# The gates of a hybrid layer in four groups of 32 columns, the first norm's sums in the same way, softplus on 144 columns, and another load order at the start

## The chip, the cores and the metric

The kernel runs on one core of one Trainium2 chip. The metric is the device time of one execution in microseconds; a run of it is repeated, and the median counts. Five engines are named: PE (matrix product), DVE (vector), ACT (scalar functions), POOL (a second, slower vector engine) and SP (which issues DMAs).

## What is computed

One inference step of a hybrid decoder layer on 576 tokens (512 of a new sequence, 64 new ones of eight older sequences), with D = 2048:

```
def _rmsnorm(x, g):
    y = xf * lax.rsqrt(jnp.mean(xf * xf, axis=-1, keepdims=True) + EPS)
    return y * g

x += W_out [GatedDeltaNet heads | mLSTM heads](RMSNorm(x) W_in)
x += ConvFFN(RMSNorm(x));  final RMSNorm
```

W_in gives q, k and v of 8 deltanet heads (each through a causal convolution of width 4 and silu), their output gates, the same for 4 mLSTM heads, and 24 rows of gates: 8 betas (sigmoid), 8 decays (softplus, times a coefficient), 4 input and 4 forget gates of the mLSTM (log-sigmoid). Everything behind the norm is float32.

## The kernel before

Tokens lie along the free axis, in two halves of 288; channels lie on the 128 partitions, so x is 16 tiles ("k") of 128x576. A float32 product is made of three faster ones: each operand is split into a high part (fp32r) and its remainder, and `three` (L193) issues high·high, high·low and low·high, each on two halves: three pairs of 128x288 matmuls for one k. `dense` (L202) does that for 16 k: one tile of 128 output channels. Its result lies in one of two "pd" buffers of PSUM until DVE has read it. Weights come in units of 128x1024 (8 k): `load_unit` (L123) issues the DMA on SP's queue, the cast to the high part on ACT (L120) and the subtraction on DVE (L121); a dense uses two units, in order of a list that begins with w_in's tile 0, the gates.

PE runs in the order in which the program is written. Beside the denses run jobs: generators that `spawn` registers. `tick`, at the end of each k of a dense, counts down every job, and where one is due lets it issue its next piece; `yield 14` means 14 k's later. So a piece of a job stands between two k's of a dense on PE. ACT, DVE, POOL and SP are ordered by a scheduler from priorities, ahead of time; each engine then keeps its order and waits where an operand is not there.

`startup` (L332) loads x on SP's queue and the parameters (par) on POOL's, makes the high and low parts of x times the norm's gain (L356 on ACT, L357 on DVE), squares x on ACT (L363) and adds the squares on DVE and POOL in turn (L365), with a last add L366. `gates` (L370) loads con (constants) and dnst (convolution states) on POOL's queue, fills small tables and runs the gate tile's dense as the first on PE, into two "pr" buffers of PSUM. Then `mixer` (L285) runs, for each head, the denses of q, k, v and z. Behind each of q, k and v stands `conv_in` (L525): an evacuation in three pieces, multiplied by rstd (L536 to L538), and the convolution (L543 to L551) on DVE with a tanh on ACT.

The job `gate_rows` (L404) goes on with the gates: 14 k's later the sum of squares over the partitions (L256, two matmuls with a matrix of ones, which also spreads it over all partitions), the reciprocal root (L244 on ACT, L245 to L248 on DVE) into rstd, the gates times rstd (L414), 6 k's later sigmoid and softplus on tiles of 128x576 (L419 to L446; the series L438 seven times, a reciprocal L432), 30 k's later the running sums, and 30 k's later the transposes L514 and L517 on PE, which turn the rows into columns for the heads. Each head is a job `dn_head` of its own (L585), which waits for the gates and the head before it; its inverse has L843 in it, its last steps L771 and its sample part L747, where four matmuls work side by side on four groups of 32 columns. L1004 in `ml_sample` does the same.

Of the kernel before, what the change touches and what calls it, by code (L numbers as in the profile page):

```python
# [19 lines left out]
NT = SEQ + NB * LS  # L20
HALF = NT // 2
# [9 lines left out]
EPS = 1e-6  # L31
# [37 lines left out]
class Layer:  # L69
# [214 lines left out]
    def mixer(self):  # L284
# [5 lines left out]
        for h in range(DNH):  # L290
            q, k, v = (self.conv_in(8 * i + h, self.dense()) for i in range(3))
# [40 lines left out]
    def startup(self):  # L332
        nc, I = self.nc, self.I
        self.par = self.cp.tile([P, NPAR], F32, tag="par", name="par")
        nc.gpsimd.dma_start(out=self.par, in_=I["par"])
# [7 lines left out]

        self.xh, self.xl = [], []
        acc = [self.r(), self.r()]
        xs = []
        acts = [self.new_act(k) for k in reversed(range(KT))][::-1]
        for k in range(KT):
            x = self.r()
            xs.append(x)  # L350
            nc.sync.dma_start(out=x, in_=I["xT"][k])
            if k in (1, 3):
                self.load_unit()
            hi, lo = acts[k]
            g = self.par[:, G1 + k:G1 + k + 1]
# [11 lines left out]
        self.acc = acc  # L367


    def gates(self):  # L370
# [3 lines left out]
        Pl.dma_start(out=self.con, in_=I["con"])  # L374
        self.ident = self.con[:, C_ID:C_ID + P]
        self.dnst = self.p1.tile([P, 24, 9, 3], F32, tag="dnst", name="dnst")
        Pl.dma_start(out=self.dnst, in_=I["dn_conv"])
# [28 lines left out]
    def gate_rows(self, outs):  # L406
        nc, I, O = self.nc, self.I, self.O
        V, A, Pl = nc.vector, nc.scalar, nc.gpsimd
        yield 14
        self.rms_bc(self.acc[0], self.rstd)  # L410
        gr = self.r()
        for hf in range(2):
            sl = slice(hf * HALF, (hf + 1) * HALF)
            V.tensor_tensor(out=gr[:, sl], in0=outs[hf], in1=self.rstd[:, sl], op=ALU.mult)  # L414
        yield 6
        edge = self.tc.issue_after(self.last_evac.ins)
        edge.__enter__()
        y = self.r()
        V.tensor_scalar(out=y, in0=gr, scalar1=self.par[:, GB:GB + 1], scalar2=self.con[:, C_SG:C_SG + 1], op0=ALU.add, op1=ALU.mult)  # L419
        R1, R2, R3 = self.r(), self.r(), self.r()  # L420
        for t in (R1, R2, R3):
            Pl.memset(t, 0.0)
        th = self.r()
        A.activation(th[0:8], gr[0:8], AF.Tanh, scale=0.5)
        V.tensor_scalar(out=R1[0:8], in0=th[0:8], scalar1=0.5, scalar2=0.5, op0=ALU.mult, op1=ALU.add)

        e = self.r()
        A.activation(e, y, AF.Abs)
        A.activation(e, e, AF.Exp, scale=-1.0)
        d = self.r()  # L430
# [1229 lines left out]
```

## Time and profile before

| what | value |
|---|---|
| median of 3 runs | 2697.02 us (2696.75 to 2697.04) |
| the profiled execution | 2699.44 us, its span 2697.70 us |
| granted TensorE clock over the span | 0.995 |
| PE busy | 2651.0 us, 98% |
| DVE busy | 1994.0 us, 74% |
| ACT busy | 1080.2 us, 40% |
| POOL busy | 333.6 us, 12% |
| data moved | 304.02 MB, 113 GB/s on the mean |

Read the shares last. PE is busy nearly throughout, so the question for any edit is in which of PE's few idle stretches it acts, and the views that show this are the list of PE's waits, the timelines of the engines at the start, and the busy times of single stretches.

### The profile page before, as it was taken

Reading aid. Unit: us, or ns where it says so; the run is one execution under the profiler, and the core shown is the slowest. Engines: PE = TensorE matmul, PEld = TensorE weight load, DVE = VectorE, ACT = ScalarE, POOL = GpSimd, SP = SyncE. Lnnn points to the kernel's source line nnn. Section 1 sums busy time; section 2 is a strip of 40 time slices with the busy share of each in tenths; the row PEclk is TensorE's granted clock in tenths of the full one; section 3 lists DMA queues with packets and bytes.
Section 4 is the critical chain, followed back from the end, with each engine's and each line's share of the span. In section 5 each row is a group of like instructions: output and inputs, shape, how many; then the busy total and the mean of one; then the engine's idle time right before and its main releaser. Section 6 shows DMA issues by size and latency. Waiting matters only on the chain.

```text
span 2697.7 us, 48872 instructions
## 1 busy us (share of the span) xinstructions
PE 2651.0 (98%) x19967; PEld 2607.0 (97%) x19967; DVE 1994.0 (74%) x3338; ACT 1080.2 (40%) x1704; POOL 333.6 (12%) x658
## 2 busy tenths in 40 slices
PE   7999999999999999998999999999999999999998
PEld 7998999999999999998999999999999999999998
DVE  7887777765544332389888888888888888888646
ACT  5334344443333322254444444444444433433324
POOL 3222322222211001101000000000000100000001
PEclk9999999999999999999999999999999999999999
DMA  5222222222333344444333333333333373342333
GB/s 195 85 77 87 90 91 91 91 88 92 114 113 104 115 135 135 135 123 150 107 111 108 108 108 108 108 108 108 108 108 109 109 256 94 106 146 71 122 97 100
DMA packets 112233, 304.02 MB, mean 113 GB/s; under 512 B 21912, under 2 KB 28184, under 8 KB 112008
## 3 DMA queue, kind: packets, MB, share of 16 engines
q1 hardware_dynamic: 107896, 291.17, 34.0%
q0 software_dynamic: 1872, 7.37, 0.8%
q8 instruction: 156, 2.56, 0.4%
q10 hardware_dynamic: 2240, 2.36, 0.3%
q14 instruction: 69, 0.57, 0.1%
HBM read 264.79 MB, written 36.06 MB: 112 GB/s over the span
## 4 chain that ended last, share of the span: by engine, by line
PE 89%; DVE 4%; DMA 1%; issue 0%; ACT 0%; POOL 0%; DVEq 0%; POOLq 0%; SPq 0%; ACTq 0%
PE pd L198 36%; PE pr L1283 31%; PE pd L1283 12%; PE pr L198 3%; PE pr L1509 1%; DVE bl L121 1%; DVE wl L121 1%; DMA r<-hid 0%; DVE r L1544 0%; PE pr L256 0%; PE pr L843 0%; PE pr L980 0%; PE pr L982 0%; PE pr L690 0%; PE pr L687 0%
## 5 line engine op out<-in xcount | busy, mean ns | idle before, releaser
L120 ACT CAST wh<-raw 128x1024 fp32r<-128x1024 f32 (+1 forms) x394 | 404.6, 1027 | 741.1 <-PE pd L198 400.2
L1283 PE MATMUL pr<-bh,wh 128*128 128x288 f32 x2120 | 626.8, 296 | 1.9 <-ACT bh L120 1.9
L1283 PE MATMUL pr<-bh,wl 128*128 128x288 f32 x2120 | 624.6, 295 | 0.5 <-DVE wl L121 0.5
L1283 PE MATMUL pr<-bl,wh 128*128 128x288 f32 x2120 | 624.3, 294 | 0.6 <-DVE bl L121 0.6
L121 DVE TENSOR_TENSOR wl<-raw,wh 128x1024 fp32r<-128x1024 f32 (+1 forms) x394 | 476.5, 1210 | 178.8 <-ACT wh L120 172.4
L198 PE MATMUL pd<-ah,wh 128*128 128x288 f32 x2496 | 560.3, 306 | 0.0
L198 PE MATMUL pd<-ah,wl 128*128 128x288 f32 x2496 | 534.5, 296 | 0.2 <-DVE wl L121 0.2
L198 PE MATMUL pd<-al,wh 128*128 128x288 f32 x2496 | 533.8, 296 | 0.0
L198 PEld LDWEIGHTS pd<-ah,wh 128*128 128x128 f32 x2496 | 401.0, 189 | 14.2 <-issue 7.7
L198 PEld LDWEIGHTS pd<-ah,wl 128*128 128x128 f32 x2496 | 401.8, 189 | 0.5 <-DVE wl L121 0.5
L198 PEld LDWEIGHTS pd<-al,wh 128*128 128x128 f32 x2496 | 401.7, 189 | 0.0
L1283 PEld LDWEIGHTS pr<-bl,wh 128*128 128x128 f32 x2120 | 400.0, 189 | 1.1 <-DVE bl L121 1.1
L1283 PEld LDWEIGHTS pr<-bh,wh 128*128 128x128 f32 x2120 | 398.4, 188 | 2.1 <-ACT bh L120 2.1
L1283 PEld LDWEIGHTS pr<-bh,wl 128*128 128x128 f32 x2120 | 398.9, 188 | 1.2 <-DVE wl L121 1.2
L120 ACT CAST wh<-s 128x1024 fp32r<-128x1024 f32 (+1 forms) x171 | 169.6, 992 | 361.2 <-DVE s L1248 142.2
L1283 PE MATMUL pd<-bh,wh 128*128 128x288 f32 x848 | 252.2, 297 | 5.6 <-ACT wh L120 5.6
L1283 PE MATMUL pd<-bh,wl 128*128 128x288 f32 x848 | 250.8, 296 | 1.7 <-DVE wl L121 1.7
L1283 PE MATMUL pd<-bl,wh 128*128 128x288 f32 x848 | 249.7, 294 | 0.0
L121 DVE TENSOR_TENSOR wl<-s,wh 128x1024 fp32r<-128x1024 f32 (+1 forms) x171 | 196.5, 1149 | 26.0 <-ACT wh L120 18.4
L1283 PEld LDWEIGHTS pd<-bh,wh 128*128 128x128 f32 x848 | 160.3, 189 | 6.1 <-ACT wh L120 6.1
L1283 PEld LDWEIGHTS pd<-bh,wl 128*128 128x128 f32 x848 | 160.6, 189 | 2.2 <-DVE wl L121 2.2
L1283 PEld LDWEIGHTS pd<-bl,wh 128*128 128x128 f32 x848 | 161.0, 190 | 0.0
(400 smaller groups left out, 3501.1 us busy)
## 6 DMA issues: line engine op xcount, KB each, us to landing
raw<-in_w_up SPq DMA_DIRECT2D x176, 512.0 KB
raw<-in_w_in SPq DMA_DIRECT2D x114, 512.0 KB
raw<-in_w_down SPq DMA_DIRECT2D x40, 512.0 KB
raw<-in_w_out SPq DMA_DIRECT2D x32, 512.0 KB
raw<-in_w_down SPq DMA_DIRECT2D x40, 384.0 KB
hid<-r SPq DMA_DIRECT2D x44, 288.0 KB
r<-hid SPq DMA_DIRECT2D x40, 288.0 KB
r<-in_xT SPq DMA_DIRECT2D x32, 288.0 KB
```

The lines of the kernel that those rows point to most:

```text
L120: nc.scalar.copy(hi, src)
L121: nc.vector.tensor_tensor(out=lo, in0=src, in1=hi.bitcast(F32), op=ALU.subtract)
L198: mm(outs[hf], w, x[:, hf * HALF:(hf + 1) * HALF], start=first and i == 0, stop=last and i == 2)
L1283: mm(out, w[:, ks], x[:, sl], start=k == 0 and i == 0, stop=k == nk - 1 and i == 2)
L1509: mm(pr[:, 0:n], w[:, ks], acts[kk][:, a * NT + sl.start:a * NT + sl.stop], start=kk == 0 and i == 0, stop=kk == FB - 1 and i == 2)
```

## The change

The gates no longer have a dense of their own. Tile 0 of w_in is read once as four float32 tiles of 128x512 (4 k's each, L371), of which POOL takes the 32 columns that matter, scaled by the norm's gain (L372), to `gw`. Their product is made in float32 on x itself, in 16 k's of four matmuls, one for each quarter of the tokens (144), into four groups of 32 output rows of one PSUM buffer (L422): inside q's dense of head 0, in blocks of four k's. Behind each k ACT squares x in place (L423). The sums of the squares are made in the same shape with 32 columns of ones (L431), in four blocks inside k's dense. The reciprocal root then runs on 128x144. One row of each group is copied to a wide tile (L436), which two matmuls with ones spread to all partitions (L452), and ACT copies that to rstd (L453). Sigmoid and softplus run on 128x144 (L465 to L487), with coefficients per group (cq, made by a small matmul L456), and two matmuls with a selection matrix (`there`, L496) bring the four groups back to rows of 576, 9 k's behind L456. For head 0, q's and k's denses now both stand ahead of the two `conv_in`. On SP's queue the first unit of q's weights stands ahead of x and the second behind four tiles of x; par, con and dnst move to this queue, and a slice of par with the norm's gain (g1) goes first on POOL's.

The core of the diff (the softplus' own steps and the memsets are left out; they are the same steps on another shape):

```diff
-        for name, n in (("w_in", NIN), ("w_out", KT), ("w_up", 2 * NPL - 2)):
-            for t in range(n):
+        for name, t0, n in (("w_in", 1, NIN), ("w_out", 0, KT), ("w_up", 0, 2 * NPL - 2)):
+            for t in range(t0, n):
...
-            q, k, v = (self.conv_in(8 * i + h, self.dense()) for i in range(3))
+            if h == 0:
+                pds = [self.dense(), self.dense()]
+                q, k = (self.conv_in(8 * i, pd) for i, pd in enumerate(pds))
+            else:
+                q, k = (self.conv_in(8 * i + h, self.dense()) for i in range(2))
+            v = self.conv_in(16 + h, self.dense())
...
-        nc.gpsimd.dma_start(out=self.par, in_=I["par"])
+        g1 = self.r(shape=[P, KT])
+        nc.gpsimd.dma_start(out=g1, in_=I["par"][:, G1:G1 + KT])
...
         for k in range(KT):
+            if k in (0, 8):
+                self.load_unit()
             x = self.r()
-            xs.append(x)
+            self.xs.append(x)
             nc.sync.dma_start(out=x, in_=I["xT"][k])
-            if k in (1, 3):
-                self.load_unit()
...
-        for k in range(KT):
-            e = nc.gpsimd if k % 2 else nc.vector
-            sq = acc[k] if k < 2 else self.r()
-            nc.scalar.activation(sq, xs[k], AF.Square)
-            if k > 1:
-                e.tensor_tensor(out=acc[k % 2], in0=acc[k % 2], in1=sq, op=ALU.add)
-        nc.vector.tensor_tensor(out=acc[0], in0=acc[0], in1=acc[1], op=ALU.add)
+            if k % 4 == 3:
+                self.gate_weights(k - 3, g1)
+        nc.sync.dma_start(out=self.par, in_=I["par"])
+
+    def gate_weights(self, k, g1):
+        raw = self.r(shape=[P, 4, 4, 32])
+        self.nc.sync.dma_start(out=raw, in_=self.I["w_in"][0][k // 8][:, k % 8 * P:(k % 8 + 4) * P].rearrange("p (k g w) -> p k g w", k=4, g=4))
+        self.nc.gpsimd.tensor_tensor(out=self.gw[:, k:k + 4].rearrange("p k (g w) -> p k g w", g=4), in0=raw[:, :, :, 0:8],
+                                     in1=g1[:, k:k + 4].unsqueeze(2).unsqueeze(3).to_broadcast([P, 4, 4, 8]), op=ALU.mult)
...
-        outs = [self.psr()[:, 0:HALF] for _ in range(2)]
-        self.dense(outs)
-        return self.spawn(self.gate_rows(outs))
+        return self.spawn(self.gate_rows())
...
-        yield 14
-        self.rms_bc(self.acc[0], self.rstd)
...
-        yield 6
+        yield 3
+        for k in range(KT):
+            for s, t in quarters:
+                mm(pg[s], self.gw[:, k], self.xs[k][:, t], start=k == 0, stop=k == KT - 1)
+            A.activation(self.xs[k], self.xs[k], AF.Square)
+            if k in (3, 7, 11):
+                yield 4
+        ps = self.psr()[:, 0:Q]
+        for k in range(KT):
+            if k % 4 == 0:
+                yield 1 if k == 0 else 4
+            for s, t in quarters:
+                mm(ps[s], self.ones[:, 0:32], self.xs[k][:, t], start=k == 0, stop=k == KT - 1)
+        self.rsqrt_bc([(ps, slice(0, Q))], 1.0 / D, self.eps6, EPS, rq[:, 0], rq[:, 1], rq[:, 2])
+        for j, (s, t) in enumerate(quarters):
+            (A.copy if j % 2 else V.tensor_copy)(wide[32 * j:32 * j + 1, t], rq[32 * j:32 * j + 1, 0])
...
+        yield 3
+        for sl in halves:
+            pr = self.psr()[:, 0:HALF]
+            mm(pr, self.ones, wide[:, sl], start=True, stop=True)
+            A.copy(self.rstd[:, sl], pr)
+        yield 4
+        pc = self.psr()
+        mm(pc[:, 0:6], back.rearrange("p j g w -> p (j g w)"), cs, start=True, stop=True)
...
-        yield 30
+        yield 9
+        for sl in halves:
+            pr = self.psr()[:, 0:HALF]
+            mm(pr, there.rearrange("p g w -> p (g w)"), t5[:, sl], start=True, stop=True)
+            A.copy(sp[:, sl], pr)
+        A.copy(R1[0:8], sp[0:8])
+        yield 5
...
-        yield 30
+        yield 26
```

Three places in the engines' orders follow. The first is ACT while x arrives: `ah` is the high part of a tile of x (ah_123 is the first, ah_93 the last), `wh` that of a unit of weights. Before, after the second cast:

```order
L120 CAST wh_147<-raw_145 128x1024
L356 ACTIVATE ah_115<-r_153,par 128x576
L356 ACTIVATE ah_113<-r_157,par 128x576
L356 ACTIVATE ah_111<-r_161,par 128x576
L356 ACTIVATE ah_109<-r_165,par 128x576
L356 ACTIVATE ah_107<-r_169,par 128x576
L356 ACTIVATE ah_105<-r_173,par 128x576
L356 ACTIVATE ah_103<-r_177,par 128x576
L356 ACTIVATE ah_101<-r_181,par 128x576
L356 ACTIVATE ah_99<-r_185,par 128x576
L363 ACTIVATE r_91<-r_125 128x576
```

After, from the second cast on:

```order
L120 CAST wh_171<-raw_169 128x1024
L541 COPY mp_900<-par 4x8
L360 ACTIVATE ah_115<-r_150,r_83 128x576
L360 ACTIVATE ah_113<-r_154,r_83 128x576
L423 ACTIVATE r_131<-r_131 128x576
L423 ACTIVATE r_135<-r_135 128x576
L423 ACTIVATE r_139<-r_139 128x576
L423 ACTIVATE r_143<-r_143 128x576
L360 ACTIVATE ah_111<-r_158,r_83 128x576
L360 ACTIVATE ah_109<-r_162,r_83 128x576
L360 ACTIVATE ah_107<-r_175,r_83 128x576
```

The four squares L423 now stand between the scalings, each behind the gate matmuls that read the same tile; before, the first square L363 came behind nine scalings of this stretch and no PE instruction.

The second place is PE at the end of head 0's k tile, with the sum's last block (16 matmuls), the two that spread the result (L452) and the first of v's dense (pd_678). Before, L256 stood a k ahead of the end of q's dense (pd_388), and k's dense (pd_528) began behind it:

```order
L198 MATMUL pd_388<-ah_95,wh_336 128x288 x2
L198 MATMUL pd_388<-al_96,wh_336 128x288 x2
L198 MATMUL pd_388<-ah_95,wl_337 128x288 x2
L256 MATMUL pr_491<-r_91,ones 128x288
L256 MATMUL pr_493<-r_91,ones 128x288
L198 MATMUL pd_388<-ah_93,wh_336 128x288 x2
L198 MATMUL pd_388<-al_94,wh_336 128x288 x2
L198 MATMUL pd_388<-ah_93,wl_337 128x288 x2
L198 MATMUL pd_528<-ah_123,wh_391 128x288 x2
L198 MATMUL pd_528<-al_124,wh_391 128x288 x2
```

After:

```order
L431 MATMUL pr_436<-r_206,ones 32x144 x4
L198 MATMUL pd_437<-ah_97,wh_344 128x288 x2
L198 MATMUL pd_437<-al_98,wh_344 128x288 x2
L198 MATMUL pd_437<-ah_97,wl_345 128x288 x2
L198 MATMUL pd_437<-ah_95,wh_344 128x288 x2
L198 MATMUL pd_437<-al_96,wh_344 128x288 x2
L198 MATMUL pd_437<-ah_95,wl_345 128x288 x2
L198 MATMUL pd_437<-ah_93,wh_344 128x288 x2
L198 MATMUL pd_437<-al_94,wh_344 128x288 x2
L198 MATMUL pd_437<-ah_93,wl_345 128x288 x2
L452 MATMUL pr_642<-r_593,ones 128x288
L452 MATMUL pr_645<-r_593,ones 128x288
```

The sum's place in PE's order moved from the end of q's dense to the end of k's.

The third place is DVE between the norm and the gates. Before, behind the reciprocal root, with q's evacuation (L536 to L538), the gates (L414, L419) and q's convolution:

```order
L246 SCALAR_TENSOR_TENSOR r_496<-rstd 128x576
L247 TENSOR_TENSOR r_496<-r_496,r_495 128x576
L248 SCALAR_TENSOR_TENSOR rstd<-r_496,rstd 128x576
L414 TENSOR_TENSOR r_504<-pr_278,rstd 128x288
L536 TENSOR_TENSOR r_513<-pd_388,rstd 128x288
L537 TENSOR_TENSOR r_513<-pd_388,rstd 128x224
L538 TENSOR_TENSOR r_513<-pd_388,rstd 128x8x8
L414 TENSOR_TENSOR r_504<-pr_279,rstd 128x288
L121 TENSOR_TENSOR wl_532<-raw_529,wh_531 128x1024
L445 TENSOR_SCALAR coef_597<-coef_597 128x1
L543 TENSOR_SCALAR r_520<-r_513,cwh 128x600
L419 TENSOR_SCALAR r_565<-r_504,par,con 128x576
```

After, with q's evacuation (L587 to L589 on pd_246), k's (pd_437) and the gates' first step (L465):

```order
L436 COPY r_593<-r_592 1x144 x2
L121 TENSOR_TENSOR wl_527<-raw_524,wh_526 128x1024
L587 TENSOR_TENSOR r_648<-pd_246,rstd 128x288
L588 TENSOR_TENSOR r_648<-pd_246,rstd 128x224
L589 TENSOR_TENSOR r_648<-pd_246,rstd 128x8x8
L594 TENSOR_SCALAR r_655<-r_648,cwh 128x600
L587 TENSOR_TENSOR r_663<-pd_437,rstd 128x288
L588 TENSOR_TENSOR r_663<-pd_437,rstd 128x224
L589 TENSOR_TENSOR r_663<-pd_437,rstd 128x8x8
L596 SCALAR_TENSOR_TENSOR r_655<-r_648,cwh,r_655 128x600
L594 TENSOR_SCALAR r_670<-r_663,cwh 128x600
L465 TENSOR_TENSOR r_713<-pr_259,r_592 128x144
```

Both evacuations, q's and k's, and both convolutions now stand ahead of or between the gates' steps, whose last, L487, is what PE's L496 reads.

## Rows read from the trace of the kernel before

**Rows 1.** The list of PE's waits, 0 to 700 us: in total, times, longest.
```profile
PE pr L198 <- ACT wh L120: 10.4, 1, 10.4
PE pr L256 <- DVE r L366: 4.3, 1, 4.3
PE pr L843 <- DVE r L836: 3.1, 1, 3.1
```

**Rows 2.** Timeline of ACT: start, us, instruction, count; in brackets idle and its releaser.
```profile
9.31 1.04 ACT L120 CAST wh<-raw 128x1024 fp32r<-128x1024 f32 x1 [2.52 <-DMA raw<-in_w_in]
...
13.48 6.51 ACT L356 ACTIVATE ah<-r,par 128x576 fp32r<-128x576 f32 x9
...
26.08 5.85 ACT L363 ACTIVATE r<-r 128x576 f32<-128x576 f32 x10
...
34.05 1.28 ACT L244 ACT_TABLE_LOAD   x1
```

**Rows 3.** Timeline of PE, 0 to 100 us.
```profile
10.41 0.85 PE L198 MATMUL pr<-ah,wh 128*128 128x288 f32 x2 [10.41 <-ACT wh L120]
...
41.76 2.29 PE L256 MATMUL pr<-r,ones 128*128 128x288 f32 x4 [4.35 <-DVE r L366]
43.43 1.09 PE L198 MATMUL pd<-ah,wh 128*128 128x288 f32 x2
...
48.07 0.43 PE L198 MATMUL pd<-ah,wh 128*128 128x288 f32 x2
...
98.46 0.60 PE L514 MATMUL pr<-con,r 128*128 128x128 f32 x4
```

**Rows 4.** Timelines of DVE and POOL: the adds of the squares.
```profile
28.20 9.63 DVE L365 TENSOR_TENSOR r<-r,r 128x576 f32<-128x576 f32 x5
...
27.48 11.60 POOL L365 TENSOR_TENSOR r<-r,r 128x576 f32<-128x576 f32 x6 [0.29 <-ACT r L363]
```

**Rows 5.** The chain of waits around 180, 652 and 221 us: start, us, what.
```profile
179.93 0.57 PE pr L747 x16
...
651.98 1.00 PE pr L1004 x16
...
221.01 0.97 PE pr L256 x4
```

**Rows 6.** Window; busy us (count) of PE, PEld, DVE, ACT, POOL; clock, DMA, GB/s.
```profile
0.00:20.00 20.00, 9.59 (x59) 9.26 (x60) 10.83 (x17) 13.07 (x19) 5.70 (x35) 1.00 0.92 341
```

**Rows 7.** Timeline of DVE, 50 to 123 us.
```profile
50.37 0.45 DVE L536 TENSOR_TENSOR r<-pd,rstd 128x288 f32<-128x288 f32 x1
...
51.03 0.21 DVE L538 TENSOR_TENSOR r<-pd,rstd 128x64 f32<-128x64 f32 x1
...
53.88 1.23 DVE L121 TENSOR_TENSOR wl<-raw,wh 128x1024 fp32r<-128x1024 f32 x1 [2.27 <-ACT wh L120]
...
55.08 0.52 DVE L543 TENSOR_SCALAR r<-r,cwh 128x600 f32<-128x600 f32 x1
...
56.01 2.60 DVE L545 SCALAR_TENSOR_TENSOR r<-r,cwh,r 128x600 f32<-128x600 f32 x3
...
62.01 3.75 DVE L432 RECIPROCAL r<-r 128x576 f32<-128x576 f32 x1
...
122.34 0.85 DVE L638 SCALAR_TENSOR_TENSOR r<-pr,cj,r 128x128 f32<-128x128 f32 x3
```

**Rows 8.** Four more windows, columns as in rows 6.
```profile
47.50:48.00 0.50, 0.50 (x4) 0.50 (x4) 0.50 (x2) 0.00 (x0) 0.00 (x0) 0.56 0.00 0
271.50:272.50 1.00, 1.00 (x11) 1.00 (x11) 1.00 (x3) 0.09 (x1) 0.43 (x1) 1.00 0.00 0
2212.00:2213.00 1.00, 0.43 (x2) 0.43 (x3) 1.00 (x3) 0.29 (x1) 0.00 (x0) 0.50 0.92 347
220.00:280.00 60.00, 54.28 (x405) 51.14 (x404) 49.50 (x118) 28.27 (x63) 21.59 (x28) 1.00 0.28 87
```

**Rows 9.** Timeline of PE at 2211 us.
```profile
2211.31 0.40 PE L1283 MATMUL pd<-bh,wh 128*128 128x288 f32 x1 [1.60 <-ACT wh L120]
```

More of the change, by code (lines that the diff above doesn't have):

```diff
@@ L400, in gates, with gate_rows @@
         Pl.memset(self.vas[:, 256:257], 1.0)
-        outs = [self.psr()[:, 0:HALF] for _ in range(2)]
-        self.dense(outs)
-        return self.spawn(self.gate_rows(outs))
-    def gate_rows(self, outs):
+        return self.spawn(self.gate_rows())
+    def gate_rows(self):
         nc, I, O = self.nc, self.I, self.O
-        V, A, Pl = nc.vector, nc.scalar, nc.gpsimd
-        yield 14
-        self.rms_bc(self.acc[0], self.rstd)
[L411 to L414, printed above, removed]
-        yield 6
+        V, A, Pl, mm = nc.vector, nc.scalar, nc.gpsimd, nc.tensor.matmul
+        Q = NT // 4
+        quarters = [(slice(32 * j, 32 * j + 32), slice(Q * j, Q * j + Q)) for j in range(4)]
+        halves = [slice(hf * HALF, (hf + 1) * HALF) for hf in range(2)]
+        pg = self.psr()[:, 0:Q]
+        yield 3
[11 more added lines that the diff above has]
+                mm(ps[s], self.ones[:, 0:32], self.xs[k][:, t], start=k == 0, stop=k == KT - 1)
+        rq, wide = self.r(shape=[P, 3, Q]), self.r()
+        Pl.memset(wide, 0.0)
+        self.rsqrt_bc([(ps, slice(0, Q))], 1.0 / D, self.eps6, EPS, rq[:, 0], rq[:, 1], rq[:, 2])
+        for j, (s, t) in enumerate(quarters):
+            (A.copy if j % 2 else V.tensor_copy)(wide[32 * j:32 * j + 1, t], rq[32 * j:32 * j + 1, 0])
+        there, back = self.r(shape=[P, 4, 32]), self.r(shape=[P, 4, 4, 8])
+        cs = self.r(shape=[P, 6])
+        for t in (there, back, cs[:, 3:6]):
+            Pl.memset(t, 0.0)
+        for j, (s, _) in enumerate(quarters):
+            Pl.tensor_copy(there[s, :, 0:8], self.ident[s, s].rearrange("p (g w) -> p g w", g=4))
+            Pl.tensor_copy(back[s, :, j], self.ident[s, 32 * j:32 * j + 8].unsqueeze(1).to_broadcast([32, 4, 8]))
+            n, v = ((3, 0.5), (5, 1.0), (4, 1.0), (5, 1.0))[j]
+            Pl.memset(cs[s, n:n + 1], v)
+        Pl.tensor_copy(cs[:, 0:2], self.par[:, GB:GB + 2])
+        Pl.tensor_copy(cs[:, 2:3], self.con[:, C_SG:C_SG + 1])
+        yield 3
[6 more added lines that the diff above has]
+        mm(pc[:, 0:6], back.rearrange("p j g w -> p (j g w)"), cs, start=True, stop=True)
+        cq = self.sm(7, "cq", 1)
+        A.copy(cq[:, 0:6], pc[:, 0:6])
@@ L416, in gate_rows @@
         edge = self.tc.issue_after(self.last_evac.ins)
         edge.__enter__()
[L418 to L425, printed above, removed]
@@ L427, in gate_rows @@
-        e = self.r()
+        c = lambda i: cq[:, i:i + 1]
+        gr, t4, t5 = self.r(shape=[P, 3, Q]), self.r(shape=[P, 3, Q]), self.r()
+        gr, y, val = (gr[:, i] for i in range(3))
+        e, d, p = (t4[:, i] for i in range(3))
+        V.tensor_tensor(out=gr, in0=pg, in1=rq[:, 0], op=ALU.mult)
+        V.tensor_scalar(out=y, in0=gr, scalar1=c(0), scalar2=c(2), op0=ALU.add, op1=ALU.mult)
+        Pl.memset(t5, 0.0)
+        A.activation(val, gr, AF.Tanh, scale=0.5)
+        V.tensor_scalar(out=val, in0=val, scalar1=c(3), scalar2=c(3), op0=ALU.mult, op1=ALU.add)
@@ L428, in gate_rows @@
         A.activation(e, y, AF.Abs)
         A.activation(e, e, AF.Exp, scale=-1.0)
-        d = self.r()
         V.tensor_scalar(out=d, in0=e, scalar1=2.0, scalar2=None, op0=ALU.add)
```

35 lines of the change are left out of this document (18 added, 17 removed).

## The prediction

> **What bounds the kernel now.** The page first: TensorE is busy 2651.0 of the 2697.7 us, so an edit can win only where PE waits. The list of PE's waits up to 700 us [rows 1] has three large ones there. PE waits 10.4 us for the first weight cast; 4.3 us at L256, the sum that gives the first norm, for the DVE add L366; and 3.1 us at L843 in the deltanet inverse. The first two are what this change works on. The ACT lines [rows 2] tell why the first is long: the first cast is done only at 10.35, and behind it ACT has nine scalings of x (6.51 for 9, so 0.72 each) and later ten squares (0.585 each). The PE lines [rows 3] place everything: the gate tile's own dense starts at 10.41 and takes some 14.5 us, q of head 0 ends at 41.76 − 4.35 = 37.41, L256 stands at 41.76, k of head 0 starts soon after, and one k into head 1's k tile stand the transposes L514, at 98.46. A dense is 16 k of three pairs; a pair's pitch is 0.267 (from 48.07 to L514 stand 189 pairs in 50.39), so a k is 0.80 and a dense 12.8. So the v tile of head 0 ends at 98.46 − 0.8 − 2 x 12.8 = **72.06**. That moment is the mark that I use: behind it PE's order is the old one but for a few steps.
>
> The adds that L366 ends are on DVE (9.63 for 5) and on POOL (11.60 for 6) at the same time [rows 4].
>
> **Part 1, the start.** Removed: 96 gate matmuls, 14 adds and L366. Added in q's dense: 16 k of four quarters of 144 columns in four groups of 32 columns, in blocks of four k. Their price is bounded by two rows of four-group work [rows 5]: L747, eight matmuls of 128 columns (16 records) in 0.57, and L1004, eight of 257 in 1.00. The slope is 0.43 for 129 columns of each of two packs, the fixed part 0.14. A block of four packs of 144 is 4 x 144 x 0.43 / 258 + 0.14 = 1.10, with the fixed part per pair of packs 1.25. I take 1.15, so 4.6 for the four blocks, against 12.8 and more for the gate dense. If the groups ran one behind another, a pack's 576 columns would cost what the sum's two matmuls of 288 cost, 0.97 [rows 5], against 0.29: +0.68 for each of 32 packs; that is a rival below.
>
> The trace shows the fixed part of such a block as 0.14 only. The Trainium skill, "TensorEngine Tiling (Array Packing)", section Tiling Modes, Key Properties, says that a change of the tiling mode drains TensorE, which speaks against eight blocks of 32-column groups set between full-width matmuls; it gives no figure. By the rows eight drains are inside the 8 x 0.14 that I have; nothing in the sum hangs on the rule.
>
> PE now starts when the first cast of q's weights is done. The weights stand ahead of x on SP's queue; the cast of 1.04 and the table load ahead of it put this at some 6.4 instead of 10.41. But then ACT is the bound, not PE: it has two casts, 16 scalings at 0.72 and, now between them, 12 of the 16 squares at 0.585 before the last scaling, since the tiles are squared in place and each square waits for its gate block on PE (the first at about 13.0). From there 12 x 0.585 + 10 x 0.72 = 14.2, so the last scaling ends at 27.2; DVE's remainder 0.78 and the last k make 28.6, and the last gate block **29.7** is the end of q. The loads are not behind this: 341 GB/s in the first 20 us [rows 6] are 6.8 MB, and the two units (0.52 each), 16 tiles of x (0.29 each), four gate tiles (0.26 each) and par (0.26) are 7.1, so the last x is there at about 21. ACT's copy of par (mp) stands ahead of the fifth scaling; par is then the ninth transfer, behind 2.5 MB, and lands at 8 to 10, when ACT has just come there (10.4).
>
> Then k's dense with four blocks of the sums: 12.8 + 4.6. **E**, its end, is 29.7 + 17.4 = **47.1** (46.5 to 48.5 by the bounds of a block). Before, k ended at 72.06 − 12.8 = 59.3. So E is 12 us ahead; but the norm and the gates now come later in the program's work than before.
>
> **Part 2, the norm.** The last block of sums stands three k ahead of E. ACT's table load 1.28 [rows 2] comes behind it, then the reciprocal root and three DVE steps on 144 columns and four row copies, some 0.28 each by the nearest row (L638, three of 128 columns in 0.85 [rows 7]): the broadcast can start at E + 0.95, a wait of 0.95. It takes 0.97, to E + 1.95. The copies that make rstd stand on ACT behind the cast wh_526 (to E + 2.0): done at E + 2.9. On DVE wl_527 (1.23) stands ahead of q's evacuation: to E + 3.2, then the evacuation, 0.87 (50.37 to 51.24 in [rows 7]), which frees v's buffer. So v starts at **E + 4.1**, a second wait of 2.15. Before, v started at 59.3 and q's evacuation was over at 51.24.
>
> **Part 3, the gates.** t5 is the end of DVE's work ahead of L496: by the order DVE has from E + 2.0 two remainders (2.4), two evacuations (1.7), two convolutions and the softplus, 22 steps of 0.28 and a reciprocal at a quarter of 3.75. A convolution is 0.52 + 2.60 and two steps that share 576 columns, some 0.9 by the 0.87 of one with 600: 4.0 [rows 7]. Sum 2.4 + 1.7 + 8.1 + 6.2 + 0.9 = 19.3; DVE's steps start some 0.08 before the one ahead ends, 14 times, so 18.0 to 18.2. t5 is at **E + 20.0**. PE comes to L496 thirteen k into v, at E + 4.1 + 10.4 = E + 14.7 with pc (L456). It waits 5.3 us. Two matmuls 0.97 and three k 2.4: v ends at E + 23.4 = **70.5**, against 72.06: −1.6. What would be late next, L565, has room: it stands 28 k behind v's end, E + 45.8, and the scans behind t5 need, as before from L456 on, about 16 us behind v's evacuation, to E + 40.
>
> **The clock.** In before the granted clock was 0.56 at 47.5 [rows 8], and nine pairs took 4.64 from 43.43 to 48.07 [rows 3]: behind the wait of 4.35. That cost 4.64 − 9 x 0.267 = 2.2 in the dense and 43.43 − 41.76 − 0.97 = 0.7 in the sum, 2.9 us that the 72.06 holds. Behind a wait of 1.60 at 2211.31 [rows 9] it was 0.50; behind the wait of 3.11 at L843 it was 1.00 (271.5 to 272.5). So a wait of 5.3 probably lowers it: I add 3.0 for v's last k and what follows. The mark then comes at 73.5: **+1.4**.
>
> **Part 4, the heads.** Softplus on 144 columns takes 13 us of DVE work out of 55 to 90, where PE had no wait: nothing. Con and dnst, moved to SP's queue, come behind all of x; POOL, which waits for con and par, has the gate weights ahead of con, and the rest due only at L456 and L496: nothing. By the order head 0's and head 2's steps stand some 5 k earlier on PE; head 1's and those from head 3 on don't move. Head 0's front: the cast wh_1242 stands ahead of L662 on ACT, +0.5 (0 to 1.5). Head 2: of the 60 us of 220 to 280 PE is idle 5.72 [rows 8], I take it since head 0's and 1's late steps and head 2's front fall together on DVE (3.1 of it at L843). With head 2's front 4 us away from head 1's steps half of this may go: −3 (0 to −5.7; above zero it can't be excluded that it comes back elsewhere, +1).
>
> Sum: +1.4 + 0.5 − 3.0 = −1.1 on the profiled run's 2699.44; on the median, which is 2.4 below, 2697.02 − 1.1, so **2696.0**. 0.2%, which is what a measurement can tell here from no change, is 5.4 us.
>
> **Rivals.** (a) No change to be told, 0.56: the 12 us won up to E are given back at v's start and at L496. For it: DVE's chain from rstd to the gates is 18 us with PE's cover of 10.4, and before PE's cover was 55 (43.43 to 98.46). (b) Faster, 0.26: the clock stays up behind L496 (−3.0) or the wait is some 3 us shorter, and head 2's stall goes whole (−2.7 more): 2696 − 5.7 − 1 (E at 46.1) = 2689. For it: the 3.11 wait that left the clock alone. Against: 4.35 and 1.60 did not. (c) Slower, 0.15: the clock falls at v's start already, behind the waits of 0.95 and 2.15 which 0.97 of the sum divides. Then v's first four k take 2.4 to 3 more, pc (L456) and with it the softplus's start come later by this, so do the casts, and the wait at L496 comes on top with a second fall. With E at 47.5 to 48.5 and head 2's stall as it was: 2696 + 3 + 3 = 2702. It decides from a fall that lasts 4 us or more before L456. (d) The groups don't run side by side, 0.03: 16 packs in q's dense, 12.8 + 16 x 0.97 = 28.3 from 6.4, end it at 34.7 instead of 29.7, and k's is 10.9 longer: +16, 2712. Against it speaks L747: eight matmuls of 128 columns in 0.57, where the sum's two of 288 are 0.97.
>
> **How the numbers follow.** Faster by over 0.2% 0.26, within 0.56, slower 0.15 + 0.03 = 0.18. The range from 2690 to 2703 takes in the clock's two outcomes, head 2's −5.7 to +1 and E's bounds, and leaves some 0.1 on each side.
>
> **What would show it.** PE's first matmul at about 6.4; q's end at 29 to 30 with ACT busy throughout; k's end near 47; PE waiting about 1 for the broadcast, 2 for DVE's evacuation ahead of v, 5 for L487 at L496; a low granted clock behind that; L365 gone; idle PE of 220 to 280 below 5.7. Wrong would be: DVE's chain from E + 2 shorter than 18 (then the wait goes and the mark is up to 5 us earlier), a block of four packs far off 1.15, or a stall in a later head that the order doesn't show.

## The result

The changed kernel takes **2708.14 us** (median of 6, 2706.22 to 2712.27), the kernel before, timed beside it, 2697.15 (6 runs): a ratio of 1.004, 95% interval [1.003, 1.0051]. It is some 11 us slower, beyond the 0.2% that can be told from no change, and above the predicted range, which ended at 2703. The profiled execution took 2712.27 us with a span of 2710.5, 12.8 us more than that of before.

In the changed kernel the heads' lines have numbers that are 51 higher: L843 is now L894, L836 L887, L834 L885, L662 L713, L562 L613, L592 L643. The list of PE's waits, 0 to 700 us (in total, times, longest), answers to [rows 1]:

```profile
PE pr L894 <- issue: 7.4, 1, 7.4
PE pd L198 <- ACT ah L360: 7.2, 2, 6.2
PE pr L496 <- DVE r L487: 4.9, 1, 4.9
```

Before's 10.4 at the start is 6.2 and the 4.3 at L256 has become 1.2 + 2.3 + 4.9. The first line is new: 7.4 us at L894, in head 0's inverse. PE begins to wait there at 151.55, 80 us behind L496, the last matmuls that the change put on PE. ("issue" is idle time for which the profile names no releaser; what L894 waits for here is the transpose L887, which starts at 158.13 and takes 0.71, as shown further down.) The timeline of PE (start, us, instruction, in brackets idle time and its releaser), which answers to [rows 3]:

```profile
6.25 0.85 PE L198 MATMUL pd<-ah,wh 128*128 128x288 f32 x2 [6.25 <-ACT ah L360]
...
30.16 0.53 PE L198 MATMUL pd<-ah,wh 128*128 128x288 f32 x2
...
35.66 1.19 PE L431 MATMUL pr<-r,ones 128*32 128x144 f32 x32
...
40.16 1.19 PE L431 MATMUL pr<-r,ones 128*32 128x144 f32 x32
...
49.63 1.24 PE L452 MATMUL pr<-r,ones 128*128 128x288 f32 x4 [1.20 <-ACT r L436]
53.17 0.82 PE L198 MATMUL pd<-ah,wh 128*128 128x288 f32 x2 [2.31 <-DVE r L589]
...
59.00 0.28 PE L456 MATMUL pr<-r,r 128*128 128x6 f32 x2
71.51 2.26 PE L496 MATMUL pr<-r,r 128*128 128x288 f32 x4 [4.94 <-DVE r L487]
...
158.95 2.05 PE L894 MATMUL pr<-r,r 128*128 128x128 f32 x8 [7.40 <-issue]
```

Windows (length; busy us and count of PE, PEld, DVE, ACT, POOL; granted clock, DMA share, GB/s), behind three of these waits and over the two stretches with the early heads; the last one answers to [rows 8]:

```profile
53.00:59.00 6.00, 5.83 (x25) 5.86 (x25) 5.48 (x10) 0.32 (x1) 2.82 (x8) 0.51 0.31 93
72.00:76.00 4.00, 4.00 (x15) 3.40 (x14) 0.14 (x1) 1.47 (x3) 0.00 (x0) 0.50 0.00 0
159.00:165.00 6.00, 6.00 (x27) 6.00 (x28) 0.00 (x0) 0.79 (x3) 2.24 (x4) 0.52 0.01 3
...
120.00:220.00 100.00, 91.39 (x701) 87.92 (x701) 73.04 (x192) 32.24 (x80) 25.82 (x42) 0.95 0.25 76
220.00:280.00 60.00, 59.45 (x460) 56.49 (x460) 46.21 (x114) 30.90 (x69) 21.29 (x27) 1.00 0.28 86
```

The stretch 120 to 220 of before:

```profile
120.00:220.00 100.00, 98.96 (x793) 94.47 (x791) 74.81 (x193) 37.36 (x87) 28.68 (x41) 1.00 0.27 83
```

**The ledger** (after minus before). Up to the end of head 0's v tile: 77.03 against 72.06, **+5.0**. Head 0's inverse: the wait 7.4, the matmuls themselves 2.05 against 1.13, and nine pairs that took 4.29 (160.65 to 164.94) where nine at full clock take 2.40: **+10.2**. Head 2's stall gone, idle 5.72 to 0.55: **−5.2**. The rest up to 340 us is −1.3, so that from there to some 1200 us the same weight cast is 8.7 to 8.8 later than before. Two boundaries of the layer, near 1240 and 2220 us, add +0.9 and +2.8 in this one execution. By the same casts the experiments' traces show +0.1 to +1.1 and −0.1 to +2.7 there, whatever they change in the gates, and before was profiled once: these 3 to 4 us are not traced to anything here, and the medians (+11.0) hold less of them than the two profiles (+12.8).

**Why head 0 is late.** The lines on head 0's chain in after, DVE first, then SP's DMA issues:

```profile
136.48 0.29 DVE L860 TENSOR_SCALAR r<-r 40x256 f32<-40x256 f32 x1 [3.84 <-DMA r<-ud]
...
153.67 0.22 DVE L885 TENSOR_TENSOR Xs<-cx,con 64x64 f32<-64x64 f32 x1 [1.07 <-DMA cx<-xd]
156.48 0.88 DVE L613 TENSOR_SCALAR r<-r,cols 128x128 f32<-128x128 f32 x4 [2.59 <-DMA r<-rowd]
...
157.43 0.67 DVE L885 TENSOR_TENSOR r<-cx,con 128x512 f32<-128x512 f32 x1
158.13 0.71 DVE L887 STREAM_TRANSPOSE r<-r 128x512 f32<-128x512 f32 x1
```

```profile
129.76 0.38 SPq L854 DMA_DIRECT2D ud<-cb  x1
131.62 0.34 SPq L129 DMA_DIRECT2D raw<-in_w_in  x1
132.06 0.31 SPq L858 DMA_DIRECT2D r<-ud  x1
...
151.62 0.38 SPq L872 DMA_DIRECT2D cx<-xd  x1
152.43 0.32 SPq L643 DMA_DIRECT2D r<-rowd  x1
```

And in before:

```profile
131.92 0.53 DVE L809 TENSOR_SCALAR r<-r 40x256 f32<-40x256 f32 x1 [0.62 <-DMA r<-ud]
...
147.58 0.88 DVE L562 TENSOR_SCALAR r<-r,cols 128x128 f32<-128x128 f32 x4 [1.38 <-DMA r<-rowd]
...
148.54 0.68 DVE L834 TENSOR_TENSOR r<-cx,con 128x512 f32<-128x512 f32 x1
...
149.27 0.69 DVE L836 STREAM_TRANSPOSE r<-r 128x512 f32<-128x512 f32 x1
```

```profile
130.08 0.31 SPq L807 DMA_DIRECT2D r<-ud  x1
131.33 8.74 SPq L129 DMA_DIRECT2D raw<-in_w_in  x2
...
144.12 0.33 SPq L592 DMA_DIRECT2D r<-rowd  x1
145.23 0.37 SPq L821 DMA_DIRECT2D cx<-xd  x1
```

The reader of r<-ud runs 4.6 us later (131.92 to 136.48): 1.6 from what comes before it, 3.0 because SP now issues the DMA right behind a unit of weights (131.62, then 132.06), and it is read 4.4 us after its issue instead of 1.8. The transpose runs 8.9 later (149.27 to 158.13). The steps of the inverse end 6.4 later (149.97 instead of 143.57), as the row of them has become 1.8 longer: the evacuation of the next tile (L587 to L589, 0.9), which before stood ahead of L809, now stands between them, where its convolution stood already. Then DVE waits 2.59 for rowd, which **head 1's** first step L613 reads, and the larger of the two instructions of head 0's L885 stands behind that wait. The step stood there before too (L562), but SP issued rowd ahead of cx then, and behind it now. PE comes to L894 1.5 us later than before, the transpose 8.9: the difference is the wait. In before there was nothing to spare: the transpose ended at 149.96, and its reader on PE started at 150.07.

Nine of the twelve experiments' traces have SP's order of after: a unit of weights some 0.4 us ahead of r<-ud, and cx ahead of rowd. There r<-ud is read 3.4 to 4.3 us after its issue, and head 0's inverse waits 3.6 to 6.8 at this matmul. Before and the other three (e1, c4 and c5 below) have the unit behind r<-ud and rowd ahead of cx: 1.7 to 1.9, and a wait of 1.5 at most. No experiment changes SP's order alone.

### The profile page after: what moved, and what is told of

Same layout as the page of the kernel before. It is cut to its first block, busy times and chain, and to the rows that moved or that the text cites. A ratio compares the mean times of both kernels' runs of the same rounds, so it can differ in the third digit from the quotient of the medians.

```text
span 2710.5 us, 49220 instructions
## 1 busy us (share of the span) xinstructions
PE 2658.2 (98%) x20133; PEld 2610.2 (96%) x20133; DVE 1972.6 (73%) x3332; ACT 1078.1 (40%) x1707; POOL 320.8 (12%) x672
## 3 DMA queue, kind: packets, MB, share of 16 engines
q8 instruction: 158, 2.59, 0.4%
## 4 chain that ended last, share of the span: by engine, by line
PE 91%; DVE 4%; DMA 2%; ACT 1%; issue 1%; POOL 0%; SPq 0%; DVEq 0%; ACTq 0%; POOLq 0%
PE pd L198 38%; PE pr L1334 31%; PE pd L1334 12%; PE pr L198 3%; PE pr L1560 1%; DMA raw<-in_w_down 1%; DMA r<-hid 1%; DVE wl L121 0%; DVE bl L121 0%; PE pr L256 0%; PE pr L894 0%; DVE r L1595 0%; PE pr L906 0%; DMA r<-in_xT 0%; PE pr L734 0%
## 5 line engine op out<-in xcount | busy, mean ns | idle before, releaser
L121 DVE TENSOR_TENSOR wl<-raw,wh 128x1024 fp32r<-128x1024 f32 (+1 forms) x392 | 470.4, 1200 | 199.5 <-ACT wh L120 193.2
```

The lines of the kernel that those rows point to most:

```text
L121: nc.vector.tensor_tensor(out=lo, in0=src, in1=hi.bitcast(F32), op=ALU.subtract)
```

## The experiments

All were timed in three rounds beside the kernel before, whose medians there were 2698.1 to 2698.8. Ratios are to it; after is at 1.004, and an interval is some ±2.7 us (±4 where a kernel has four runs: e2, f3 and g2), so differences below 4 us between two kernels rest on their traces. Added lines move the numbers: L894 is L895 to L909 in some kernels, L496 is L497 or L501.

**Head 0's steps put back five k's (e1).**

```diff
-        yield 26
+        yield 31
         nc.sync.dma_start(out=self.rowd[0:8], in_=G[32:40])
```

> The changed kernel with one number other: the transposes L565 (and with them all of head 0's and head 2's steps) 5 k's later on PE, where they stood before the change. Theory A: the changed kernel loses 5.0 us up to the end of head 0's v tile and some 10 more at L894 in head 0's inverse (a wait of 7.4 and slow matmuls behind it), because head 0's steps stand 4 us earlier on PE than DVE can serve them; it gets 5.2 back in head 2. Then here the wait at L894 falls to 0 to 1.5 and the clock stays up there, and head 2's idle time of some 5 us at 220 to 280 comes back: 10 less, 5 more, about 2703. Theory B: the wait at L894 comes from what DVE and the DMA queues do at that time (head 1's work ahead of the transpose), wherever PE stands: 7.4 becomes 3.4, and with 5 in head 2 back the time is as the changed kernel's, 2707 to 2709.

2705.06 us, 1.0022 [1.0012, 1.0032], some 5 us below after. Head 0's L894 waits 1.5 instead of 7.4, the clock of 120 to 220 is back at 1.00, and head 2's stall is back (L894 on PE, then windows):

```profile
157.05 1.13 PE L894 MATMUL pr<-r,r 128*128 128x128 f32 x8 [1.51 <-issue]
...
120.00:220.00 100.00, 97.50 (x772) 93.08 (x771) 74.12 (x194) 36.00 (x96) 26.35 (x39) 1.00 0.26 81
220.00:280.00 60.00, 55.99 (x426) 52.69 (x425) 47.24 (x116) 32.52 (x68) 22.33 (x30) 1.00 0.27 86
```

So the place of the heads' steps, an edit of one number, carries some 5 of the 11 us by the medians, and 3.3 of 8.7 by the weight casts at 600 us, where L496's wait is 1.1 longer (6.05): 10 us at head 0 were paid for 5 at head 2.

**The matrix that brings the gates back (L496) seven k's later, the heads where they were (e2).**

```diff
-        yield 9
+        yield 16
         R1, R2, R3 = self.r(), self.r(), self.r()
...
-        yield 26
+        yield 19
```

> The changed kernel with the matmuls L496 7 k's (5.6 us) later on PE, in z's dense instead of v's; L565 stays where it is. Theory A: the wait of 4.94 for DVE's L487 goes, and the low clock behind it (2.2 us in the two matmuls and five pairs) too: 7 less, about 2701. Theory B: what follows L496 is on the path as well (the running sums up to L565 and the heads), so the wait comes back at L565 or grows at L713 and L894: 2706 to 2709.

2709.15 us, 1.0038 [1.0023, 1.0053]: nothing won, theory B's time, though the wait stayed at L496 itself.

```profile
78.11 2.26 PE L496 MATMUL pr<-r,r 128*128 128x288 f32 x4 [6.01 <-DVE r L487]
```

PE waits 6.0 at L496, now at 78.11: the last gate step, L487, begins at 77.24 instead of 70.64, because the scheduler put v's evacuation and convolution ahead of it on DVE. Cover on PE alone doesn't help where DVE's order moves with it.

**The sums of squares earlier in k's dense, so that rstd is there when v starts (e3).**

```diff
-                yield 1 if k == 0 else 4
+                yield 1 if k == 0 else 2
...
-        yield 3
+        yield 6
         for sl in halves:
...
-            A.copy(self.rstd[:, sl], pr)
-        yield 4
+            with self.urgent():
+                A.copy(self.rstd[:, sl], pr)
+        yield 7
```

> The changed kernel with the four blocks of the sums (L431) two k's apart instead of four, the matmuls that spread the result three k's ahead of k's end instead of at it, and the copies to rstd ahead of the weight cast on ACT. Everything behind keeps its place counted from v's start. Theory A: PE's waits ahead of v (1.2 and 2.3) go, the clock stays up there (12 pairs at 0.48 instead of 0.267, 2.6 us); DVE's chain starts some 4 us earlier against k's end, PE comes to L496 6 earlier, so the wait there grows from 4.9 to 7: 4 less, about 2704. Theory B: the end of DVE's chain alone decides and it starts no earlier, since DVE has the same work in front of it: all of it is found again at L496, 2707 to 2709.

2704.25 us, 1.0018 [1.0009, 1.0028], some 6 us below after. The waits of 1.2 and 2.3 ahead of v are gone and v starts at full clock; L497 waits 6.8 and L895 still 6.6.

**The two together, with L496 twelve k's later and the heads five k's later than in after (c4).** The sums as above, and `yield 9` to 21, `yield 26` to 19.

> The sums early as in the third kernel, L496 12 k's later than in the changed kernel and the transposes L565 5 k's later, as before the change. Theory A: no wait ahead of v and none at L496, k of head 0 ends at 48, v at 62 to 63 where it ended at 72.06 before the change: 9.3 less than the kernel before, head 0 and head 2 as before the change (5.7 idle at the place of 220 to 280): 2688, 2685 to 2691. Theory B: the time won at the start is waited for in head 0's front, since DVE's chain from the gates to the columns and the heads is as long as it was: 2695 to 2699.

2693.88 us, 0.9986 [0.9977, 0.9995]: 15 us below after, and below before; between the two theories. PE still waits 2.2 at L497; head 2's stall is there as in before (55.93 busy of 60 from 220 to 280), with 1.5 at L709 and 1.5 at L895 in it.

**The gates' chain first on DVE: head 0's convolutions of q and k behind its last step, and L456 right behind the broadcast (f1).**

```diff
+        if t in (0, 8):
+            self.convs = getattr(self, "convs", []) + [lambda: self.conv(t, rb, h)]
+            return rb
...
-        yield 4
         pc = self.psr()
...
+        yield 4
...
+        with self.tc.issue_after(last.ins):
+            for f in self.convs:
+                f()
```

> The changed kernel with the convolutions of q and k of head 0 ordered behind the gates' last step L487 on DVE, and the small matmul L456 right behind the norm instead of four k's into v. In the kernel with L496 moved seven k's later the wait at L496 stayed (6.0), because DVE took v's evacuation and convolution ahead of the gates' last steps. Theory A: it is DVE's order alone that makes PE wait at L496; with the gates first DVE has some 10 us from the evacuations to L487 instead of 17, PE doesn't wait at L496 and the clock stays up there: 7 less than the changed kernel, some 0.14 to 0.2 per cent above the kernel before. Theory B: the 8 us of convolutions that are moved back are waited for later (v's evacuation, the running sums, the columns L565 or head 0's front): as the changed kernel.

2700.46 us, 1.0006 [0.9997, 1.0016], some 9 below after. The list of PE's waits has no line for L496 any more:

```profile
PE pr L905 <- issue: 6.5, 1, 6.5
PE pd L198 <- DVE r L592: 2.1, 1, 2.1
```

The wait at L496 is DVE's order, not PE's: with the convolutions out of the way the gates are done in time. The second half of the edit has a part in this: L466 reads what L456 makes, and begins at 54.14 here, ahead of the 59.00 at which L456 stood in after. The two halves were not run apart. Head 0's stall stays at 6.5 with gates that are ready earlier.

**The squares of x behind the last scaling on ACT (f2)**, to see what bounds the start.

```diff
-            A.activation(self.xs[k], self.xs[k], AF.Square)
+            with self.tc.issue_after(self.last_ah.ins):
+                A.activation(self.xs[k], self.xs[k], AF.Square)
```

> The changed kernel with all squares L423 behind the last scaling L360 on ACT. Theory A: q's dense is bound by ACT, which has 12 squares of 0.585 between the scalings; with them behind, the last scaling comes some 6 us earlier, with the last tile of x, q's dense ends at 25 instead of 30.9, and k's, whose sums have the squares in time, at 42.5 instead of 48.4; everything behind comes 6 earlier: 6 less than the changed kernel. Theory B: the loads of x bind at once (its last tile lands at 21 to 24) or the squares make the sums wait in k's dense: 0 to 2 less.

2707.72 us, 1.0029 [1.0018, 1.0041]; not told apart from after. The last scaling ends at 23.15 instead of 27.4, but k's dense ends only 0.7 earlier, at 47.7, and v starts 1.0 earlier, at full clock. Q's dense ends 2.4 earlier, at 27.7, and PE has no wait in it behind 8.30; but k's first k then waits 0.96 for its weight cast, which now stands behind eight squares on ACT, and 0.46 for the remainder on DVE. So ACT's order is worth 2.4 us in q's dense, and this edit moves most of it into k's:

```profile
52.19 0.50 PE L198 MATMUL pd<-ah,wh 128*128 128x288 f32 x2 [2.31 <-DVE r L590]
52.53 0.42 PE L198 MATMUL pd<-al,wh 128*128 128x288 f32 x2
```

and it is waited for in full:

```profile
70.52 2.26 PE L497 MATMUL pr<-r,r 128*128 128x288 f32 x4 [7.51 <-DVE r L488]
```

From v's start to L496's it is 18.33 here and 18.34 in after (53.17 to 71.51), though here v's first twelve pairs cost 2.6 less. DVE's chain sets L496; the clock at v's start doesn't.

**Head 0's inverse (L894) nine k's later (f3).**

```diff
-YZ = 5
+YZ = 14
```

> The changed kernel with the second half of head 0's inverse, from L894 on, 9 k's (7.2 us) later on PE; all ahead of it as it was. Theory A: L894's wait of 7.4 goes and with it the low clock behind it (1.2 in L894 itself and about 2.4 in the next pairs); the steps of head 0 behind it come 7 us later, and of head 2's gain of 5.2 some part goes: 6 to 11 less than the changed kernel. Theory B: what is late is not this step but all of head 0's and head 1's DVE work, so the wait comes again at the next steps (L906, L708, L713, L822): 0 to 3 less.

2718.93 us, 1.0074 [1.0059, 1.0089], some 9 us worse, against both theories. Head 0's L894 waits 3.9 instead of 7.4, but L894 of a later head waits 6.0, and L713 4.6 in three places; PE is busy 52.85 of 60 from 280 to 340, against 60.00 in after. Cover given to one step comes back as waits of the steps behind it and of later heads.

**All of the start's repairs (c5)**: early sums, gates first, squares late, L496 18 k's behind L456 (`yield 7`, then 11), which is 15 k's into v, and the heads five k's later than in after against v's start (two by L496's place, three by `yield 26` to 29).

> The kernel with the sums early, the gates first on DVE, the squares behind the scalings, L496's pair of matmuls 15 k's into v and the columns L565 where they stood before the change. Theory A: PE has no wait from its second k to head 0's front; k of head 0 ends at 42.5 and v at 56 to 57 with the pair in it, where v ended at 72.06 before: head 0 and head 2 then wait as before the change, so 12 to 14 less than the kernel before. Theory B: head 0's front has DVE's convolutions, running sums and columns ahead of it, which don't come earlier by as much, and waits for them: 5 to 8 less than the kernel before.

2693.25 us, 0.998 [0.997, 0.9989], some 5 us below before: theory B. Head 0's L907 waits 0.2 and head 2's stall is there (55.94 busy of 60).

**Head 1 a little later, so that its L613 no longer stands ahead of head 0's L885 (g1).**

```diff
         sl4 = slice(SEQ, NT)
+        if h == 1:
+            yield 4
...
-        yield YS if h == 0 else 9
+        yield YS if h == 0 else 5 if h == 1 else 9
```

> Edit: as the kernel after, but head 1's decay stage begins four k's later, so that on DVE head 0's second half of the inverse (L887) is no longer ordered behind head 1's L613, which waits for a DMA of rowd. Theory A: that wait (2.6 us of the 7.4 at head 0's L894, in the kernel after) passes through DVE to PE. Then L894 waits some 4 us to 5 us instead of 7.4, and the time falls by 3 to 4 us, to about 0.4% minus 0.13% over the kernel before (2705.5). Rival B: the wait at L894 is set by the chain of head 0 (cumulative lateness of r<-ud and the steps behind it) whatever L613 does: the wait stays at 6.5 to 7.5 and the time within 1.5 us of the kernel after (2708 to 2710).

2704.17 us, 1.0019 [1.001, 1.0029], some 6 below after. DVE, where L887, L889 and L896 are after's L885, L887 and L894:

```profile
152.46 0.69 DVE L887 TENSOR_TENSOR r<-cx,con 128x512 f32<-128x512 f32 x1 [1.16 <-DMA cx<-xd]
...
153.21 0.70 DVE L889 STREAM_TRANSPOSE r<-r 128x512 f32<-128x512 f32 x1
...
155.85 0.88 DVE L613 TENSOR_SCALAR r<-r,cols 128x128 f32<-128x128 f32 x4 [1.95 <-DMA r<-rowd]
```

L613 still waits for rowd, but head 0's steps no longer stand behind it. The transpose is 4.9 earlier, of which PE too is 1.2 earlier in this trace, and PE's wait is 3.7 instead of 7.4. Head 2's stall stays away (59.26 busy of 60). Half of head 0's wait is another head's step and its DMA, through DVE's order. The other half goes with r<-ud's trip, 4.3 us here as in after, and the longer row of steps; no experiment took these away alone.

**The heads two k's later (g2).**

```diff
-        yield 26
+        yield 28
```

> Edit: as the kernel after, but the heads' steps on PE stand two k's (1.6 us) later (26 to 28). Theory A: head 0's chain on DVE, SP and ACT is fixed by what comes before it, so PE is simply too early; two k's more of cover take 1.6 us of the 7.4 at L894, and the time is 1.6 lower, about 2707.5. Rival B: what counts is where the weight units' DMAs and head 1's steps fall against head 0's chain. Then two k's change the wait by something else: below 4 us or above 9 us, and the time by more than 3 us in either direction.

2717.85 us, 1.0074 [1.0059, 1.0089], some 9 us worse. L894's first wait falls to 5.4, by about what theory A said, but later heads now stall:

```profile
281.54 1.56 PE L894 MATMUL pr<-r,r 128*128 128x128 f32 x8 [4.11 <-DVE r L887]
```

PE is busy 55.73 of 60 from 220 and 56.58 from 280, and the clock of 280 to 340 is 0.94. Two k's later is worse and five k's later is better, so the cover alone doesn't decide. That it is which step of one head meets which of the next is how I read it; for these later heads it was not followed to its end. Theory A was right on its wait and wrong on the time.

**c5 with its heads five k's earlier (g3)** (`yield 29` to 24).

> Edit: as the best kernel (all starts and gates in new places, c5), but the heads' steps on PE five k's earlier (29 to 24). There no wait at L496 or at L894 is above 1.6 us, and the gates are ready early. Theory A: head 0's stall at L894 comes from the place of its steps among the weight units and head 1's steps, not from late gates: it then returns with 5 us to 7 us, the granted clock of 120 to 220 falls to some 0.95 and the time is 5 to 9 us above c5 (2698 to 2702). Rival B: it comes from the gates being late: with the gates early the heads can start five k's earlier without a wait over 2 us, and the time stays within 2 us of c5 (2691 to 2695).

2694.96 us, 0.9987 [0.9978, 0.9997].

```profile
PE pr L907 <- issue: 6.6, 1, 6.6
```

The stall of 6.6 at head 0 returns though the gates are early here: it comes from the place of the steps. The time is only 1.7 above c5, which the intervals don't tell from no change, since head 2's stall goes in exchange (59.23 busy of 60 against 55.94): theory A on the wait, B on the time.

**g3 with head 1 a little later (g4)**, the edit of g1.

> Edit: g3 (gates early, heads' steps five k's earlier than in c5) with g1's edit (head 1's decay stage begins four k's later). Theory A: the two effects are separate and add: g3's stall of 6.6 us ahead of L907/L909 falls to about 3 us, head 2's stall (window 220 to 280) stays away at 59 us or more of PE busy, and the time is 3 to 5 us below g3, 2690 to 2692. Rival B: head 1 four k's later meets head 2 again, and what the first stall gives is taken back in 220 to 280 or 280 to 340: PE busy there falls by 3 us or more and the time stays at 2694 to 2697.

2690.74 us, 0.9974 [0.9964, 0.9984], the fastest here; before, timed beside it, was 2698.06.

```profile
PE pr L909 <- issue: 3.6, 1, 3.6
```

```profile
220.00:280.00 60.00, 59.40 (x456) 56.66 (x455) 48.56 (x116) 24.83 (x59) 22.42 (x28) 1.00 0.31 99
```

Head 0's wait falls by 3.0, head 2's stall stays away, and the two effects add. It is some 17 us below after and 7 below before, with the same four-group gates.

## Why the prediction was wrong

**The step that failed is Part 4, "Head 0's front: ... +0.5 (0 to 1.5)".** It measured +10.2. The prediction priced one cast on ACT ahead of L662. The stall is later, at L894, and is made of two DMA trips, a neighbour head's step that waits for a DMA ahead of head 0's on DVE, and the low clock behind the wait. All of these are in the orders of SP and DVE behind the front, and the sum has no term for them. The other half of the same edit was right: head 2's stall went, −5.2 (predicted −3, down to −5.7). So an edit that was counted as −2.5 in all was +5. The first experiment (e1), g1, g3 and g4 show it: the wait goes with the place of the steps, comes back with it though the gates are early, and loses half with head 1's step.

**Part 1 held, with the block mis-sized.** PE starts at 6.25 (6.4). A block of 16 small matmuls takes 1.12 to the next pair and makes that pair slower; from L431 to L431, 4.50 less 12 pairs of 0.267 (3.20) is **1.30**, above the 1.15 taken and the bound 1.25. The groups do run side by side (rival d falls). Q ends at 30.16 (29.7), k at 48.43 (E = 47.1): +1.3. That ACT bounds this stretch held for q's dense (the last scaling ends at 27.4, 27.2 forecast), but it is worth only 2.4 us there: with the squares out of the way (f2) PE goes without a wait from 8.30 and ends q at 27.7.

**Part 2 held.** Waits of 1.20 and 2.31 (0.95 and 2.15), v at E + 4.7 (4.1).

**Part 3 had the right wait for a wrong sum.** PE waits 4.94 at L496 (5.3), but L496 runs at E + 23.1 where t5 was put at E + 20.0. DVE's lines show where the 3 us are:

```profile
52.15 0.45 DVE L587 TENSOR_TENSOR r<-pd,rstd 128x288 f32<-128x288 f32 x1
...
55.54 2.55 DVE L594 TENSOR_SCALAR r<-r,cwh 128x600 f32<-128x600 f32 x1
...
67.96 1.33 DVE L479 SCALAR_TENSOR_TENSOR r<-r 128x144 f32<-128x144 f32 x4
...
70.64 1.50 DVE L487 SCALAR_TENSOR_TENSOR r<-r,cq 32x144 f32<-32x144 f32 x4
```

One convolution step of 0.53 took 2.55, the short steps some 0.33 (1.33 for four) to 0.38 (1.50 for four) instead of 0.28, and the chain from the evacuation to L487's end 20.0 instead of 16.8. The long step is not the most of it: in g1's, f3's and g2's traces it took 0.53, and the chain there is 18.7 to 18.8. The other 1.9 to 2.0 lie, as far as the lines show, in the short steps and in a wait of 0.52 for POOL ahead of the first L594 that the sum didn't have. That the wait came out as forecast was luck: PE was late too, by the clock.

**The clock.** Rival (c) was right that it falls at v's start already: twelve pairs took 5.83 (53.17 to 59.00), 2.6 too long. It was wrong that this costs: f2 has these 2.6 back and waits for them at L496. Behind L496 the low clock cost 2.2 (3.0 predicted). The prediction's row for a wait of 1.60 [rows 9] left out that a second one, of 0.73, follows it two matmuls later: the granted clock of 2211 to 2212, between the two, was 0.99, and it was 0.50 only behind the second. So it is the same case as v's start, and it spoke for (c). Together the end of v is +5.0 where +1.4 was forecast: E 1.3 and DVE's chain 3.1 more, the clock 0.8 less.

**The rivals.** (a), no change, was what I held likeliest and fell by 11 us. (b) had head 2's stall going whole, which it nearly did, and the wrong sign. (c) named the right sign and a clock that fell, but not what cost the time. (d) fell with the 1.30 of a block, where four packs of 0.97 would be 3.9. None of the four had head 0. Its mechanism, a moved step that meets a DMA of the next head, has no part in the "+0.5 (0 to 1.5)". L843 of head 0 had no wait in before, but only just, as shown above.

## What to carry to other kernels

When an edit shifts jobs by a few steps, follow each moved chain to its end on every queue, DMA issues included, and note how much slack its last step had before; a step without a wait may have had next to nothing to spare (0.1 us here). An engine that keeps a fixed order passes a neighbour's DMA wait on to whoever stands behind it, so look for a waiting instruction of another chain between two of yours. And test a shift at more than one size: two k's were 9 us worse here, five k's 5 us better.

## What the runs showed of the hardware

- The granted clock fell to 0.50 to 0.52, the lower of its two levels, behind waits of PE of 4.94 and 7.40, and behind 1.20 and 2.31 with two matmuls between, and stayed there for 4.5 to 5.8 us of work. Behind a wait of 3.67 it fell too (g1: L896 took 2.05 like L894 in after). Behind a single wait of 3.11 in before pairs kept their full pace, and in f2 behind 0.93 and 2.31. In f1, behind 1.22 and 2.10 with L456's small matmul also between, five pairs kept it, and then the clock was 0.51 from 54.60 to 57.80. In after each of the three stalls that brought it down cost some 2 to 3 us more than its own length.
- A DVE step of 128x600 took 2.55 us where others of its line took 0.53. POOL's memsets L467 and L492 began 0.09 us behind it and ended at 57.77, the step at 58.09. In g1 the first memset began 0.10 behind the step, and it came out the other way: the step took 0.53, and the memset 0.95 instead of 0.58. In each of e1, e2, e3, f2 and c4 the longest such step (1.8 to 2.6) ran beside POOL's memsets too. So by the traces one of the two waits for the other in this pair of steps; no edit was made to test it. The lines of after, then of g1:

```profile
55.63 0.58 POOL L467 MEMSET r<- 128x576 f32 x1
56.15 1.62 POOL L492 MEMSET r<- 128x576 f32 x3
```

```profile
56.02 0.53 DVE L594 TENSOR_SCALAR r<-r,cwh 128x600 f32<-128x600 f32 x1
...
56.12 0.95 POOL L467 MEMSET r<- 128x576 f32 x1
```

- A small DMA (r<-ud) was read 3.4 to 4.4 us after its issue in the ten traces where SP had issued a unit of weights some 0.4 us ahead of it, and 1.7 to 1.9 us in the four where the unit came behind it.
- The Trainium skill, "TensorEngine Tiling (Array Packing)", section Tiling Modes, Key Properties, says that a change of the tiling mode drains TensorE. The block's 1.30 against the 0.96 that its columns cost by the slope of [rows 5] leaves 0.34 for going in and out, more than the 0.14 that those rows gave. The trace agrees that such a switch has a price; that the 0.34 is all of it was not tested.
